# Probability-by-value product of the prompt attention: one head's high and low value columns as one stationary block, two matmuls per key tile in place of three

## Chip, cores and metric

The kernel runs on one core of one Trainium2 chip. The metric is device time in microseconds (us), from the first to the last instruction of one launch; the median of three runs before the change is 2038.55 us.

## What is computed

Two layers of a streaming encoder over 544 frames: 512 of a new prompt stream and 32 of a running stream. Each layer has a short convolution and a latent attention side by side, a gated merge, and a SwiGLU feed-forward part. The part that the change touches is the attention of the 512 prompt frames: 16 heads, 64 value columns each, masked in chunks of 64.

```python
kv = (c_all @ w_ukv).reshape(bsz, n_keys, N_HEADS, QK_NOPE + V_HEAD)
k_nope, v = kv[..., :QK_NOPE], kv[..., QK_NOPE:]
...
s = (jnp.einsum('bqhn,bkhn->bhqk', q_nope, k_nope)
     + jnp.einsum('bqhr,bkr->bhqk', q_rope, k_rope))
s = s.astype(jnp.float32) * ATTN_SCALE
mask = (k_pos // CHUNK)[None, :] <= (q_pos // CHUNK)[:, None]
s = jnp.where(mask[None, None], s, jnp.float32(NEG_INF))
p = jax.nn.softmax(s, axis=-1).astype(v.dtype)
return jnp.einsum('bhqk,bkhv->bqhv', p, v)
```

## The kernel before

Features lie on the 128 partitions and frames along the free axis, in two halves of 272 frames. Every float32 operand of a matmul is split into a high part of reduced precision (fp32r) and a low part that holds the rest. `split` (lines 128 to 130) does it in two steps: ScalarE copies the source into the high part, which rounds it, and VectorE subtracts that from the source into the low part. `mm3` (lines 183 to 186) then makes a product of three matmuls, low by high, high by low and high by high, all summed in one bank of PSUM.

One layer runs in stages: the input projection, the attention of the prompt frames with the convolution units woven in, the attention of the sample frames, the merge, and the feed-forward part. The order on TensorE, SyncE and GpSimd is the order in which the program is written. In the attention stages the order on VectorE and ScalarE is chosen by a scheduler when the program is built. An engine takes its instructions in order, so one that waits holds up all behind it.

The stage at hand is the loop over 16 heads (lines 781 to 805). For a head `k` the program issues on TensorE:

- `attn_s` for the query tiles 0 and 1 (scores of 128 queries by 256 keys), one `fill()`, then `attn_s` for the query tiles 2 and 3 (384 and 512 keys). `fill()` issues a unit of other work, 24 matmuls of 272 columns of a convolution or gate projection. The scores lie in the PSUM tiles `ps_s`, of which there are two, taken in turn. The softmax of a query tile goes: VectorE maximum (line 739), ScalarE exponential (742), VectorE reciprocal (744) and scaling (745) into a tile `pr`.
- `attn_t(0)`: three transposes of `pr` blocks into a bank `ps_t`; the first needs the scaled `pr` of query tile 1. `split` takes them to `pth` and `ptl`, the high and low parts of the transposed probabilities.
- in some heads, work for heads to come: `attn_v(k // 4)` (values of four heads), `prep_k`, `attn_group`; then `fill()`.
- `attn_t(1)` and `attn_t(2)`, four and three transposes, each followed by its `split`; in odd heads `prep_q` for the next pair; for the heads in `H` (line 448) another `fill()`. Heads 8 and 15 have nothing between `attn_t(2)` and the product.
- `attn_pv(k)` (lines 759 to 772), the product of probabilities and values. Two query pairs of 256 queries, of two and four key tiles; each of these six tiles is an `mm3`, 18 matmuls of 256 columns. The stationary block is the 128 columns of a pair of heads, of which only the 64 of head `k` are used: ScalarE copies those 64 partitions out of the bank `ps_v` into `at`.

```python
jj = (j % 2) * P
mm3(pv[:, qp * 256 : qp * 256 + 256], v[:, 0, kt, jj : jj + P], v[:, 1, kt, jj : jj + P],
    pth[:, b, o : o + 256], ptl[:, b, o : o + 256], kt == 0, kt == nkt - 1)
s = slice(64 * i, 64 * i + 64)
act.copy(at[0][s, j, :], pv[s, :TH])
act.copy(at[1][s, j, :PB], pv[s, TH:])
```

`attn_v(r)` (lines 686 to 699) makes the values of four heads for four key tiles: two banks `ps_d`, each with two key tiles of 256 columns, and one `split` of 512 columns for each bank. The banks `ps_d` are three and are taken in turn by all units in this stage, so a unit waits until the bank of the third unit before it has been read. Ahead of the head loop the order is `attn_v(0)`, two `fill()` units, `prep_k(0)`, `prep_q(0)`.

The pool `tp` (tag `t`) has six buffers for `pr` and other short-lived tiles.

Of the kernel before, what the change touches and what calls it, by code (L numbers as in the profile page):

```python
# [33 lines left out]
def kernel(  # L34
# [42 lines left out]
    def blk(shape, dt=F32, s="b"):  # L77
        return bp.tile(shape, dt, tag="b", name=nm(s))
# [49 lines left out]
    def split(hi, lo, src, eng_hi=None):  # L128
        act.copy(hi, src)  # L129
        dve.tensor_sub(lo, src, f32(hi))  # L130
# [52 lines left out]
    def mm3(ps, whi, wlo, xhi, xlo, first, last):  # L183
        pe.matmul(ps, lhsT=wlo, rhs=xhi, start=first, stop=False)  # L184
        pe.matmul(ps, lhsT=whi, rhs=xlo, start=False, stop=False)  # L185
        pe.matmul(ps, lhsT=whi, rhs=xhi, start=False, stop=last)  # L186
# [266 lines left out]
    for l in range(NL):  # L453
# [231 lines left out]

        def attn_v(r):
            wa = prep(w_a[l, r, :, 384:896], 512)
            v = blk([P, 2, 4, 256], F32R, "v")
            for t2 in range(2):
                ps = psd(512)  # L690
                for t in range(2):
                    tt = 2 * t2 + t
                    for k in range(2):
                        o = k * 256
                        mm3(ps[:, t * 256 : t * 256 + 256], c[:, 0, k, tt * P : tt * P + P], c[:, 1, k, tt * P : tt * P + P],
                            wa[:, 0, o : o + 256], wa[:, 1, o : o + 256], k == 0, k == 1)
                pr = ps.rearrange("p (t n) -> p t n", t=2)
                split(v[:, 0, 2 * t2 : 2 * t2 + 2, :], v[:, 1, 2 * t2 : 2 * t2 + 2, :], pr)
            vs[r] = v

        wbs = {}
# [57 lines left out]
        def attn_pv(k):  # L759
            j, i = k // 2, k % 2  # L760
            v = vs[j // 2]
            pv = bank("v")
            jj = (j % 2) * P
            for qp in range(2):
                nkt = 2 + 2 * qp
                for kt in range(nkt):
                    b, o = TB[(qp, kt)]
                    mm3(pv[:, qp * 256 : qp * 256 + 256], v[:, 0, kt, jj : jj + P], v[:, 1, kt, jj : jj + P],
                        pth[:, b, o : o + 256], ptl[:, b, o : o + 256], kt == 0, kt == nkt - 1)
            s = slice(64 * i, 64 * i + 64)  # L770
            act.copy(at[0][s, j, :], pv[s, :TH])
            act.copy(at[1][s, j, :PB], pv[s, TH:])

        attn_group(0)
        fill(F[2])
# [421 lines left out]
```

## Time and profile before

| what | us |
|---|---|
| runs (three) | 2038.04, 2038.55, 2038.92; median 2038.55 |
| span of the profiled execution | 2039.1 |
| TensorE busy in the span | 2012.5 (99%) |
| VectorE busy | 1126.1 (55%) |
| ScalarE busy | 826.2 (41%) |
| head loop of layer 0, about 115 to 353 us | 238 |
| head loop of layer 1, about 1127 to 1365 us | 238 |

The profiled execution's own time is its span, 2039.1 us, 0.55 us above the median of the runs. The busy time of an engine is the time in which at least one of its instructions was open. Matmuls overlap each other, so the pace of TensorE is read from the distance between the starts of neighbouring matmuls, not from their durations.

### The profile page before, as it was taken

Reading aid. Unit: us, or ns where it says so; the run is one execution under the profiler, and the core shown is the slowest. Engines: PE = TensorE matmul, PEld = TensorE weight load, DVE = VectorE, ACT = ScalarE, POOL = GpSimd, SP = SyncE. Lnnn points to the kernel's source line nnn. Section 1 sums busy time; section 2 is a strip of 40 time slices with the busy share of each in tenths; the row PEclk is TensorE's granted clock in tenths of the full one; section 3 lists DMA queues with packets and bytes.
Section 4 is the critical chain, followed back from the end, with each engine's and each line's share of the span. In section 5 each row is a group of like instructions: output and inputs, shape, how many; then the busy total and the mean of one; then the engine's idle time right before and its main releaser. Section 6 shows DMA issues by size and latency. Waiting matters only on the chain.

```text
span 2039.1 us, 37704 instructions
## 1 busy us (share of the span) xinstructions
PE 2012.5 (99%) x15780; PEld 1995.1 (98%) x15780; DVE 1126.1 (55%) x2330; ACT 826.2 (41%) x1692; POOL 89.6 (4%) x212
## 2 busy tenths in 40 slices
PE   8999999999999999999999999999999999999997
PEld 8999999999999999999999999999999999999997
DVE  7876775533457444432668776755334664444224
ACT  5455555622354222322444555546133533322231
POOL 0101000000000000000101100000000000000000
PEclk9999999999999999999999999999999999999998
DMA  5122222222342222233532222222223412222233
GB/s 190 63 76 67 68 71 78 80 97 94 106 148 95 73 93 84 84 92 90 183 104 77 64 64 74 82 73 92 94 83 115 157 66 83 92 88 88 78 113 125
DMA packets 58891, 190.93 MB, mean 94 GB/s; under 512 B 7970, under 2 KB 9666, under 8 KB 58594
## 3 DMA queue, kind: packets, MB, share of 16 engines
q1 hardware_dynamic: 49104, 163.58, 24.6%
q0 software_dynamic: 8320, 22.66, 3.4%
q8 instruction: 123, 2.02, 0.4%
q10 hardware_dynamic: 1296, 2.29, 0.3%
q14 instruction: 48, 0.38, 0.1%
HBM read 174.11 MB, written 10.20 MB: 90 GB/s over the span
## 4 chain that ended last, share of the span: by engine, by line
PE 93%; DVE 3%; DMA 1%; ACT 1%; issue 1%; SPq 0%; DVEq 0%; ACTq 0%
PE ps_d L184 16%; PE ps_d L186 16%; PE ps_d L185 16%; PE ps_s L184 7%; PE ps_s L186 7%; PE ps_s L185 7%; PE ps_t L184 6%; PE ps_t L186 6%; PE ps_t L185 6%; PE ps_t L755 2%; PE ps_v L185 1%; DMA raw<-in_w_in 1%; PE ps_v L186 1%; PE ps_v L184 1%; DVE w L130 1%
## 5 line engine op out<-in xcount | busy, mean ns | idle before, releaser
L130 DVE TENSOR_TENSOR w<-raw,w 128x1024 fp32r<-128x1024 f32 (+4 forms) x317 | 363.7, 1148 | 431.6 <-ACT w L129 429.5
L129 ACT CAST w<-raw 128x1024 fp32r<-128x1024 f32 (+4 forms) x317 | 312.1, 986 | 271.0 <-PE ps_d L186 107.8
L184 PE MATMUL ps_d<-hh,w 128*128 128x272 f32 x1080 | 315.2, 292 | 0.2
L185 PE MATMUL ps_d<-hl,w 128*128 128x272 f32 x1080 | 312.2, 289 | 0.8 <-DVE hl L314 0.8
L186 PE MATMUL ps_d<-hh,w 128*128 128x272 f32 x1080 | 312.4, 289 | 0.0
L184 PE MATMUL ps_d<-gh,w 128*128 128x272 f32 x704 | 205.9, 292 | 6.0 <-DVE w L130 5.8
L185 PEld LDWEIGHTS ps_d<-hl,w 128*128 128x128 f32 x1080 | 203.8, 189 | 2.0 <-DVE hl L314 1.3
L184 PEld LDWEIGHTS ps_d<-hh,w 128*128 128x128 f32 x1080 | 203.9, 189 | 1.5 <-PE ps_s L186 0.6
L186 PE MATMUL ps_d<-gh,w 128*128 128x272 f32 x704 | 204.4, 290 | 0.0
L186 PEld LDWEIGHTS ps_d<-hh,w 128*128 128x128 f32 x1080 | 203.4, 188 | 0.0
L185 PE MATMUL ps_d<-gl,w 128*128 128x272 f32 x704 | 203.4, 289 | 0.0
L184 PEld LDWEIGHTS ps_d<-gh,w 128*128 128x128 f32 x704 | 133.2, 189 | 6.5 <-DVE w L130 6.2
L184 PE MATMUL ps_s<-gh,w 128*128 128x272 f32 x464 | 136.9, 295 | 1.6 <-DVE w L130 1.6
L186 PE MATMUL ps_s<-gh,w 128*128 128x272 f32 x464 | 136.1, 293 | 0.0
L185 PE MATMUL ps_s<-gl,w 128*128 128x272 f32 x464 | 135.4, 292 | 0.0
L185 PEld LDWEIGHTS ps_d<-gl,w 128*128 128x128 f32 x704 | 133.5, 190 | 0.0
L186 PEld LDWEIGHTS ps_d<-gh,w 128*128 128x128 f32 x704 | 133.1, 189 | 0.0
L184 PE MATMUL ps_t<-gh,w 128*128 128x272 f32 x432 | 125.5, 291 | 0.0
L186 PE MATMUL ps_t<-gh,w 128*128 128x272 f32 x432 | 125.0, 289 | 0.0
L185 PE MATMUL ps_t<-gl,w 128*128 128x272 f32 x432 | 124.4, 288 | 0.0
L1045 ACT ACTIVATE sl<-sl 128x272 f32<-128x272 f32 x88 | 38.0, 432 | 182.9 <-DVE sl L1044 182.9
L1053 ACT CAST fh<-sl 128x272 fp32r<-128x272 f32 x88 | 36.9, 420 | 162.8 <-DVE sl L1051 162.8
(331 smaller groups left out, 5492.0 us busy)
## 6 DMA issues: line engine op xcount, KB each, us to landing
raw<-in_w_in SPq DMA_DIRECT2D x91, 512.0 KB, 3.4
raw<-in_w_gu SPq DMA_DIRECT2D x88, 512.0 KB, 3.3
raw<-in_w_mix SPq DMA_DIRECT2D x48, 512.0 KB, 3.2
raw<-in_w_dn SPq DMA_DIRECT2D x36, 512.0 KB, 3.6
raw<-in_w_dn SPq DMA_DIRECT2D x18, 384.0 KB, 3.1
raw<-in_w_b SPq DMA_DIRECT2D x16, 320.0 KB, 2.8
x_mid<-xb POOLq DMA_DIRECT2D x16, 272.0 KB, 2.3
xb<-x_mid POOLq DMA_DIRECT2D x16, 272.0 KB, 4.9
```

The source lines that it names most:

```text
L129: act.copy(hi, src)
L130: dve.tensor_sub(lo, src, f32(hi))
L184: pe.matmul(ps, lhsT=wlo, rhs=xhi, start=first, stop=False)
L185: pe.matmul(ps, lhsT=whi, rhs=xlo, start=False, stop=False)
L186: pe.matmul(ps, lhsT=whi, rhs=xhi, start=False, stop=last)
L755: pe.transpose(pt[:, o * P : o * P + P], probs[qt][:, kt * P : kt * P + P], ident)
L1045: act.activation(sl, sl, AF.Silu)
L1053: act.copy(fh[:, i % 8, :], sl)
```

## The change

The values of a head are laid out so that its 64 high and 64 low columns stand side by side: high then low for even heads, low then high for odd ones. This block of 128 columns is the stationary operand of both matmuls of a key tile, one over `ptl` and one over `pth`, so that four partial products (with low by low, which was left out before) come out of two matmuls. The high-column results lie on the same 64 partitions as before, the low-column results on the other 64. ScalarE copies the low 64 partitions, all 512 columns, to a new tile `rest` on the head's own partitions; VectorE adds `rest` to the high half in PSUM, in two pieces, into `at`. The first matmul of each key tile now reads `ptl`. In `attn_v` the split of a bank is done in two halves of 256 columns, one for each key tile.

```diff
         def attn_v(r):
             wa = prep(w_a[l, r, :, 384:896], 512)
-            v = blk([P, 2, 4, 256], F32R, "v")
+            v = blk([P, 4, 8, 64], F32R, "v")
+            vq = v.rearrange("p t (q a) d -> p t q a d", q=2)
             for t2 in range(2):
                 ps = psd(512)
...
-                pr = ps.rearrange("p (t n) -> p t n", t=2)
-                split(v[:, 0, 2 * t2 : 2 * t2 + 2, :], v[:, 1, 2 * t2 : 2 * t2 + 2, :], pr)
+                for t in range(2):
+                    pr = ps[:, t * 256 : t * 256 + 256].rearrange("p (q e d) -> p q e d", q=2, e=2)
+                    split(vq[:, 2 * t2 + t, :, 0::3, :], vq[:, 2 * t2 + t, :, 1:3, :], pr)
             vs[r] = v
...
             pv = bank("v")
-            jj = (j % 2) * P
+            a = 2 * (k % 4)
             for qp in range(2):
                 nkt = 2 + 2 * qp
                 for kt in range(nkt):
                     b, o = TB[(qp, kt)]
-                    mm3(pv[:, qp * 256 : qp * 256 + 256], v[:, 0, kt, jj : jj + P], v[:, 1, kt, jj : jj + P],
-                        pth[:, b, o : o + 256], ptl[:, b, o : o + 256], kt == 0, kt == nkt - 1)
-            s = slice(64 * i, 64 * i + 64)
-            act.copy(at[0][s, j, :], pv[s, :TH])
-            act.copy(at[1][s, j, :PB], pv[s, TH:])
+                    both = v[:, kt, a : a + 2, :]
+                    out = pv[:, qp * 256 : qp * 256 + 256]
+                    pe.matmul(out, lhsT=both, rhs=ptl[:, b, o : o + 256], start=kt == 0, stop=False)
+                    pe.matmul(out, lhsT=both, rhs=pth[:, b, o : o + 256], start=False, stop=kt == nkt - 1)
+            s, low = slice(64 * i, 64 * i + 64), slice(64 - 64 * i, P - 64 * i)
+            rest = tmp([P, NP], s="rest")
+            act.copy(rest[s, :], pv[low, :])
+            dve.tensor_add(at[0][s, j, :], pv[s, :TH], rest[s, :TH])
+            dve.tensor_add(at[1][s, j, :PB], pv[s, TH:], rest[s, TH:])
```

The scheduler gives VectorE and ScalarE another order with it. Two places matter below.

The first is VectorE at the beginning of head 2 of layer 0, with the last step of head 1. Line numbers after `attn_v` are shifted by 2 and, behind `attn_pv`, by 6: the maximum is L739 before and L741 after, the reciprocal L744 and L746, the scaling L745 and L747. Before:

```order
L739 TENSOR_REDUCE y_1690<-ps_s_237_1686 128x1
L744 RECIPROCAL y_1695<-y_1693 128x1
L739 TENSOR_REDUCE y_1702<-ps_s_242_1698 128x1
L745 TENSOR_SCALAR pr_1692<-pr_1692,y_1695 128x128
L744 RECIPROCAL y_1707<-y_1705 128x1
L745 TENSOR_SCALAR pr_1704<-pr_1704,y_1707 128x256
L604 TENSOR_TENSOR z_843<-cv_1537,ps_d_247_1710 128x240
L605 TENSOR_TENSOR z_843<-cv_1537,ps_d_247_1710 128x32
L739 TENSOR_REDUCE y_1741<-ps_s_248_1737 128x1
```

And after the change:

```order
L741 TENSOR_REDUCE y_1686<-ps_s_239_1682 128x1
L130 TENSOR_TENSOR slot_106_835<-ps_d_236_1649,slot_106_835 64x240
L777 TENSOR_TENSOR at_1114<-ps_v_237_1665,rest_1678 64x272
L778 TENSOR_TENSOR at_1115<-ps_v_237_1665,rest_1678 64x240
L746 RECIPROCAL y_1691<-y_1689 128x1
L741 TENSOR_REDUCE y_1698<-ps_s_244_1694 128x1
L747 TENSOR_SCALAR pr_1688<-pr_1688,y_1691 128x128
L604 TENSOR_TENSOR z_843<-cv_1537,ps_d_249_1706 128x240
L605 TENSOR_TENSOR z_843<-cv_1537,ps_d_249_1706 128x32
L746 RECIPROCAL y_1703<-y_1701 128x1
L741 TENSOR_REDUCE y_1737<-ps_s_250_1733 128x1
L747 TENSOR_SCALAR pr_1700<-pr_1700,y_1703 128x256
```

The two additions stand behind the maximum of query tile 0, and the scaling of query tile 1 (128x256) has moved from in front of the maximum of query tile 2 to behind it. That last move is found in heads 2, 6, 8, 12, 13 and 14 of both layers; in the other ten the scaling still stands in front.

The second is VectorE ahead of the head loop of layer 0, behind `attn_v(0)`, where the first bank is `ps_d_158` and `xr` is rotated in the lines 422 to 425. Before:

```order
L423 TENSOR_TENSOR sh_1144<-sh_1144,sinT 128x544
L424 TENSOR_TENSOR xr_1121<-xr_1121,cosT 128x544
L130 TENSOR_TENSOR v_1164<-ps_d_158_1165,v_1164 128x512
L130 TENSOR_TENSOR v_1164<-ps_d_159_1180,v_1164 128x512
L130 TENSOR_TENSOR w_1331<-raw_1330,w_1331 128x1024
L425 TENSOR_TENSOR xr_1121<-xr_1121,sh_1144 128x544
```

And after the change:

```order
L130 TENSOR_TENSOR v_1164<-ps_d_158_1165,v_1164 128x2x128
L423 TENSOR_TENSOR sh_1144<-sh_1144,sinT 128x544
L424 TENSOR_TENSOR xr_1121<-xr_1121,cosT 128x544
L130 TENSOR_TENSOR v_1164<-ps_d_159_1182,v_1164 128x2x128
L130 TENSOR_TENSOR w_1335<-raw_1334,w_1335 128x1024
L130 TENSOR_TENSOR v_1164<-ps_d_158_1165,v_1164 128x2x128
L425 TENSOR_TENSOR xr_1121<-xr_1121,sh_1144 128x544
```

The last read of the first bank now stands behind the subtraction for a weight tile (`w`, 1024 columns); before, it stood in front of it.

## Rows read from the trace of the kernel before

**Rows 1.** Page: span, TensorE's busy time, granted clock in 40 slices.

```profile
span 2039.1 us, 37704 instructions
...
PEclk9999999999999999999999999999999999999998
```

**Rows 2.** Groups of TensorE: count, busy us, mean ns of one, idle before.

```profile
L185 PE MATMUL ps_v<-ptl,v 128*128 128x256 f32 x192 | 54.7, 285 | 1.2 <-DVE ptl L130 1.2
```

**Rows 3.** Timeline of TensorE, head 2 of layer 0: start us, duration us.

```profile
146.97 0.28 PE L184 MATMUL ps_v<-pth,v 128*128 128x256 f32 x1
...
149.12 0.28 PE L184 MATMUL ps_s<-slot 128*128 128x256 f32 x1
```

**Rows 4.** Waits of TensorE, 60 to 400 us: total us, times, longest.

```profile
PE ps_d L185 <- DVE hl L314: 0.8, 2, 0.4
PE ps_v L185 <- DVE ptl L130: 0.6, 2, 0.3
PE ps_s L184 <- ACT prs L850: 0.3, 1, 0.3
```

**Rows 5.** Windows: the head loop of layer 0, and the beginning of layer 1.

```profile
115.00:353.00 238.00, 237.41 (x1836) 232.49 (x1835) 166.96 (x386) 131.97 (x335) 20.88 (x52) 1.00 0.24 72
...
1060.00:1120.00 60.00, 59.50 (x445) 58.48 (x445) 48.07 (x123) 27.63 (x60) 5.41 (x18) 0.94 0.20 65
```

**Rows 6.** Groups of ScalarE and VectorE by shape, 115 to 353 us.

```profile
L771 ACT COPY at<-ps_v 64x272 f32<-64x272 f32 x16 | 6.1, 380 | 18.3 <-PE ps_v L186 18.3
L772 ACT COPY at<-ps_v 64x240 f32<-64x240 f32 x16 | 5.7, 354 | 0.0
...
L129 ACT CAST v<-ps_d 128x512 fp32r<-128x512 f32 x6 | 3.5, 587 | 2.6 <-PE ps_d L186 2.6
...
L130 DVE TENSOR_TENSOR slot<-ps_d,slot 64x272 fp32r<-64x272 f32 x14 | 6.1, 436 | 1.5 <-ACT slot L129 1.3
...
L130 DVE TENSOR_TENSOR slot<-ps_d,slot 64x240 fp32r<-64x240 f32 x14 | 5.6, 402 | 0.3
```

**Rows 7.** Timelines of TensorE, then VectorE, head 14 of layer 0.

```profile
330.13 0.34 PE L184 MATMUL ps_s<-slot 128*128 128x384 f32 x1
...
331.36 0.38 PE L755 MATMUL ps_t<-ident,pr 128*128 128x128 f32 x2
...
328.79 0.41 DVE L739 TENSOR_REDUCE y<-ps_s 128x1 f32<-128x256 f32 x1
329.12 0.28 DVE L745 TENSOR_SCALAR pr<-pr,y 128x128 f32<-128x128 f32 x1
...
330.09 0.35 DVE L745 TENSOR_SCALAR pr<-pr,y 128x256 f32<-128x256 f32 x1
330.86 0.56 DVE L739 TENSOR_REDUCE y<-ps_s 128x1 f32<-128x384 f32 x1 [0.41 <-PE ps_s L186]
```

**Rows 8.** Timelines of TensorE, then VectorE, head 8 of layer 0.

```profile
242.27 0.36 PE L184 MATMUL ps_v<-pth,v 128*128 128x256 f32 x1
...
243.65 0.38 PE L185 MATMUL ps_v<-ptl,v 128*128 128x256 f32 x1 [0.30 <-DVE ptl L130]
243.87 0.28 PE L186 MATMUL ps_v<-pth,v 128*128 128x256 f32 x1
...
245.06 0.28 PE L184 MATMUL ps_s<-slot 128*128 128x256 f32 x1
...
242.90 1.16 DVE L130 TENSOR_TENSOR ptl<-ps_t,pth 128x512 fp32r<-128x512 f32 x2 [0.67 <-ACT pth L129]
```

**Rows 9.** Timelines of TensorE, then VectorE, ahead of the head loop of layer 0.

```profile
96.32 0.29 PE L184 MATMUL ps_d<-hh,w 128*128 128x272 f32 x1
...
93.52 0.70 DVE L423 TENSOR_TENSOR sh<-sh,sinT 128x544 f32<-128x544 f32 x1
...
94.80 1.27 DVE L130 TENSOR_TENSOR v<-ps_d,v 128x512 fp32r<-128x512 f32 x2
95.99 1.20 DVE L130 TENSOR_TENSOR w<-raw,w 128x1024 fp32r<-128x1024 f32 x1
```

## The prediction

> **What bounds the kernel now.** I read the page first. TensorE is busy almost all of the 2039.1 us, and its granted clock stands at the upper of its two levels, 2.4 GHz, in nearly every slice [rows 1]. So what counts is TensorE's pace and its waits, and other engines only where TensorE waits for them. Next the groups by line: the product of probabilities and values is 192 matmuls of 256 columns for each of the three partial products [rows 2]. Their duration of 285 ns is not their price, since they overlap. The timeline of one head gives that: from the first of its 18 matmuls to the first of the next scores 149.12 - 146.97 = 2.15 us pass, 0.119 us for each [rows 3]. Then the waits of TensorE: from 60 to 400 us it waited less than 2 us in all, and one of the three rows lies inside the product, 0.3 us in each of two heads, for the last low parts of the probabilities [rows 4]. Last the window of the head loop: VectorE is the next engine, busy 167.0 of 238 us, ScalarE 132.0 [rows 5]. VectorE has room on average, so the question is whether it is late at the one moment when TensorE needs it.
>
> **The change part by part.**
>
> Removed: one matmul of three for 6 key tiles, 16 heads and 2 layers, that is 192 [rows 2]. At 0.119 us each [rows 3] this is 192 x 0.119 = **22.9 us** (2.15 / 3 = 0.72 us per head). Ends: the pace is a measured one for just this shape, so I allow 22 to 23.5.
> The Trainium skill has another price: "TensorE: Matmul & The Clock Gate", section "Back-to-back issue gap", gives a stream of weight load and matmul pairs 81 ns at 128 columns and 131 ns at 512; an estimate on the straight line between them is 98 ns at 256 columns, with which the matmuls would be worth 18.8 us and the sum below would be 18.8 - 5.8 - 1.4 - 1.5 = 10.1 us gained, about 2028.4. The row of this case, 0.119 us, does not agree and decides.
>
> Evictions of the product: ScalarE gives up two copies of 0.380 and 0.354 us [rows 6] and does one of 64x512, for which the nearest row is 0.587 us (128x512 out of PSUM). VectorE gets two additions with one operand in PSUM; the nearest rows, subtractions of the same shapes, take 0.436 and 0.402 us [rows 6], a little less than 0.8 us a head, under 13 us a layer. VectorE has 238 - 167 = 71 us free [rows 5], so I cost them at nothing as work. The copy moves data to other partitions, which no row shows; its bounds are nothing extra and twice the 0.587. ScalarE's copy and the additions read `ps_v`, whose next use is a head later, about 15 us: nothing there either way. If that cover went, for example because VectorE was late by 1 us in every head, the softmax behind it would be the one to tell.
>
> That is where the order of VectorE counts. In head 2 as in heads 6, 8, 12, 13 and 14 of both layers, 12 places, the scaling of query tile 1 now stands behind the maximum of query tile 2 (front, first place). The first transpose needs that scaling. Head 14 shows the times [rows 7]: the scores of query tile 2 start at 330.13, their maximum can start only at 330.86, and TensorE wants the transpose at 331.36. The scaling was started at 330.09 and was long done. Now it starts when the maximum lets go: rows of such pairs show the next instruction start 0.08 us before the end of the one before (328.79 + 0.41 against 329.12), so 330.86 + 0.56 - 0.08 = 331.34, and it ends at 331.34 + 0.35 = 331.69. TensorE is late by 0.33 us, plus the resumption: in head 8 a matmul that had waited was followed after 0.22 us (243.65 to 243.87) [rows 8], not 0.119, so 0.10 more, and 0.05 for the signal, which I estimate from the same row (243.65 is a few hundredths behind the end of the first of the two subtractions). Together 0.48 us, 12 x 0.48 = **5.8 us lost**. Ends: 12 x 0.33 = 4.0 without resumption; 12 x 0.85 = 10.2 if VectorE has another 0.37 us of backlog there (about one addition). I take the middle one because the maximum itself waits for TensorE, which swallows backlog before it.
>
> Heads 8 and 15 of both layers have no cover between the last transposes and the product. In head 8 the product starts at 242.27 and stops until 243.65, 1.38 us later, for the low part [rows 8]. The new order reads that low part with the first matmul of the third key tile, and 1.38 us is still when it is there. Before, 11 matmuls were left (243.65 to 245.06), now 8. So this head saves 3 x 0.119 = 0.36 us and not 0.72: 4 x 0.36 = **1.4 us lost**. Ends: nothing, if VectorE is earlier there, and 0.72 each, 2.9 us, if it is later by 0.36.
>
> Values: each bank is split in two halves. The copy of 512 columns takes 0.587 us and one of 272 columns 0.380 [rows 6], so a split bank costs ScalarE some 0.15 us more, VectorE likewise; in heads 4, 8 and 12 other units of TensorE cover that. Ahead of the head loop they don't: the second half of the first bank is now read behind the subtraction of a 1024-column weight tile (front, second place). From 93.52 [rows 9]: one half about 0.34, the two rotations 94.80 - 93.52 = 1.28, another half 0.34, the weight tile 1.2, the second half 0.42; the bank is free at about 97.1, and the second `fill()` unit, third in turn on this bank, was started at 96.32. That is 0.75 us with the signal, in each layer: **1.5 us lost**. Ends: nothing, if the weight tile's subtraction waits less than I think and the half goes first in time, and 2.4 us, if ScalarE's second copy is late by another 0.45.
>
> The rest of each layer keeps its instructions and only starts earlier. SyncE's and GpSimd's order is the same as before apart from buffer names, and the weight transfers wait for the buffers that VectorE and ScalarE free, so they move with the rest. The new tile `rest` takes one of six buffers of `tp`; the buffers it presses on hold `pr` tiles that the transposes have released before the product starts, so I cost it at nothing, up to 2 us.
>
> **The sum.** 22.9 - 5.8 - 1.4 - 1.5 = 14.2 us gained. On the profiled execution, 2039.1, that is 2024.9; the median of the runs is 0.55 lower, so **2024.4 us**, 0.7% less. TensorE's clock falls to its lower level, 1.2 GHz, for short stretches at the layers' beginnings (the window at 1060 us shows 0.94 [rows 5]); if layer 1 begins 7 us earlier these may fall otherwise, and I leave 2 us to both sides for it. A difference of 0.2%, 4 us, is about what a measurement of this kernel can tell from no change.
>
> **Rivals.**
>
> *The scaling is never late*: the maximum or the transposes shift so that the 5.8 us don't appear. For it speaks that VectorE has 30% of the loop free; against it that the maximum of query tile 2 can't start before its scores, and that this leaves 0.50 us (330.86 to 331.36) for 0.83 us of work [rows 7]. Time: 2024.4 - 5.8 = 2018.6.
>
> *VectorE is late in more heads*: its additions, which wait for the end of the product and ScalarE's copy, stand in front of the reciprocal and maximum of query tile 1 in 30 heads. If half the heads lose another 0.4 us to it at the transposes or in front of the product, 16 x 0.4 = 6.4 us, the time is 2030.8. For it: the low parts decide already in four heads. Against: the scaling of query tile 1 ended at 330.44, 0.9 us ahead of its transpose [rows 7].
>
> *Slower than before*: the copy across partitions and the additions become the bound of the softmax. It decides from the point where every head loses over 0.72 us at its first transpose; the scaling of query tile 1 has 0.9 us to spare in head 14 [rows 7], so it would have to come over 1.6 us later. The additions bring 0.8 of that, so the copy would have to take over 0.8 us more than the 0.587 of its nearest row. With 2.0 us for it the scaling comes 0.8 + 1.4 = 2.2 us later, a head loses 2.2 - 0.9 = 1.3 us and saves 0.72: 32 x 0.58 = 18.6 us slower, 2057.
>
> *It does not do what it says*: the matmuls go but TensorE's time is taken by something that hides behind them, and nothing over 0.2% is left. Against it: the loop's 0.6 us of idle time in 238 [rows 5]. Time: 2036.
>
> **How the numbers follow.** My forecast, 2021 to 2028, has a chance of 0.62; the scaling never late 0.12; more heads late 0.18; no gain to speak of 0.05; slower 0.03. The range from 2018 to 2031 takes in the first three cases: at the lower end 5.8 us of waits fall away, at the upper the transposes' wait is at its 10.2 and the other bounds at theirs, 22.9 - 10.2 - 2.9 - 2.4 = 7.4, 2031.2. Faster by over 0.2%: 0.92; within 0.2%: 0.05; slower: 0.03.
>
> **What the profile would show.** Right: 192 matmuls fewer, still 0.119 us apart; waits of TensorE at line 757 (the transposes) for VectorE's scaling, some 0.3 us each in 12 places; four waits of a product's low-part matmul, longer than 0.3 us; one wait of a `fill()` unit in front of the head loop for the subtraction of `v`, 0.7 us, in each layer; VectorE busier by 12 us a loop, the head loop some 7 us shorter. Wrong: no waits at line 757, or such waits in nearly all heads; new waits at `ps_s` for the exponential; or a loop whose matmuls are further apart.

## The result and the profile after

The changed kernel takes 2023.38 us (median of 4 runs, 2021.93 to 2026.63), against 2038.74 of the kernel before in the same comparison: a ratio of 0.9923, interval 0.9909 to 0.9937, 15.4 us less. The forecast was 2024.4, in a range from 2018 to 2031. The profiled execution is the longest of the four; its span, from the first to the last instruction in the profile, is 2024.6 us and its time 2026.63. The part ahead took a span for the time of a run; where a run has both on record, the time is 1.7 to 2.9 us more. The forecast does not hang on this, since 2024.9 - 0.55 is the median of the runs before, 2038.55, less the 14.2 of the sum.

The waits of TensorE over its whole span are the first view (us in total, times, longest), to be held against [rows 4]:

```profile
PE ps_v L772 <- DVE ptl L130: 2.5, 4, 0.7
...
PE ps_t L757 <- DVE pr L747: 1.6, 8, 0.2
PE ps_d L184 <- DVE v L130: 1.3, 2, 0.7
...
PE ps_s L184 <- ACT pr L744: 0.4, 2, 0.2
```

The first three are the three waits of the forecast: the product for the low parts in heads 8 and 15, the transposes for VectorE's scaling, the unit ahead of the loop for the values. Each comes in both layers; at the transposes there are eight waits of 0.2 us and not twelve of 0.3. The fourth is new: it is in head 14 of each layer, and the forecast had named such waits, of `ps_s` for the exponential, as a sign of being wrong. The groups of 115 to 345.7 us, by shape, answer to [rows 2, 6]:

```profile
L772 PE MATMUL ps_v<-ptl,v 128*128 128x256 f32 x96 | 24.0, 286 | 1.3 <-DVE ptl L130 1.3
L773 PE MATMUL ps_v<-pth,v 128*128 128x256 f32 x96 | 23.7, 282 | 0.0
...
L776 ACT COPY rest<-ps_v 64x512 f32<-64x512 f32 x16 | 9.3, 582 | 11.1 <-PE ps_v L773 10.7
L777 DVE TENSOR_TENSOR at<-ps_v,rest 64x272 f32<-64x272 f32 x16 | 6.9, 434 | 1.5 <-ACT rest L776 1.4
L778 DVE TENSOR_TENSOR at<-ps_v,rest 64x240 f32<-64x240 f32 x15 | 6.0, 397 | 0.0
```

The copy to other partitions, which no row showed before, takes 582 ns, about as long as its nearest row (587). The additions take 434 and 397, as the subtractions of the same shapes (436 and 402). VectorE and TensorE in head 14 of layer 0, the counterpart of [rows 7]:

```profile
322.68 0.42 DVE L741 TENSOR_REDUCE y<-ps_s 128x1 f32<-128x256 f32 x1
323.02 0.28 DVE L747 TENSOR_SCALAR pr<-pr,y 128x128 f32<-128x128 f32 x1
323.80 0.16 DVE L746 RECIPROCAL y<-y 128x1 f32<-128x1 f32 x1 [0.50 <-ACT pr L744]
323.88 0.54 DVE L741 TENSOR_REDUCE y<-ps_s 128x1 f32<-128x384 f32 x1
324.33 0.34 DVE L747 TENSOR_SCALAR pr<-pr,y 128x256 f32<-128x256 f32 x1
```

```profile
322.95 0.34 PE L184 MATMUL ps_s<-slot 128*128 128x384 f32 x1
...
323.82 0.50 PE L184 MATMUL ps_s<-slot 128*128 128x512 f32 x1 [0.19 <-ACT pr L744]
...
324.73 0.55 PE L757 MATMUL ps_t<-ident,pr 128*128 128x128 f32 x3
325.03 0.37 PE L184 MATMUL ps_d<-hh,w 128*128 128x272 f32 x1
```

From the scores of query tile 2 to the transposes 324.73 - 322.95 = 1.78 us pass; before it was 1.23 [rows 7]. The scaling ends at 324.67, and the transposes start 0.06 us later, as the forecast has it. But the rows show one more wait, that of the scores of query tile 3 (128x512) for the exponential of query tile 1: these matmuls take the bank that the exponential reads. Head 14 is the exception: the same distance is 1.59 or 1.60 us in heads 2, 6, 8, 12 and 13 of both layers, and 1.22 in the other ten. Head 8, TensorE, answers to [rows 8]:

```profile
238.33 0.36 PE L772 MATMUL ps_v<-ptl,v 128*128 128x256 f32 x1
...
239.65 0.39 PE L772 MATMUL ps_v<-ptl,v 128*128 128x256 f32 x1 [0.60 <-DVE ptl L130]
239.87 0.28 PE L773 MATMUL ps_v<-pth,v 128*128 128x256 f32 x1
...
240.70 0.28 PE L184 MATMUL ps_s<-slot 128*128 128x256 f32 x1
```

The product starts 3.94 us earlier than before and the next scores 4.36, so this head saves 0.42 us and not 0.72. Ahead of the loop, VectorE and TensorE, beside [rows 9]:

```profile
95.24 1.20 DVE L130 TENSOR_TENSOR w<-raw,w 128x1024 fp32r<-128x1024 f32 x1
...
96.38 0.41 DVE L130 TENSOR_TENSOR v<-ps_d,v 128x256 fp32r<-128x256 f32 x1
```

```profile
96.93 0.36 PE L184 MATMUL ps_d<-hh,w 128*128 128x272 f32 x1 [0.66 <-DVE v L130]
```

The second half of the first bank is read behind the weight tile, and the unit starts at 96.93; before it was 96.32, in a run that had come to this place 0.2 us later.

**How kernels are compared below.** The whole times of one kernel's runs lie up to 7.2 us apart (`e_third_back`, 2038.69 to 2045.9). Windows of two profiled executions of the changed kernel show why (the column in front of the last two is TensorE's mean granted clock), first of the one above, then of its repetition `c_after`:

```profile
1060.00:1080.00 20.00, 20.00 (x139) 20.00 (x139) 17.31 (x55) 5.95 (x12) 0.46 (x4) 0.83 0.01 1
```

```profile
1060.00:1080.00 20.00, 20.00 (x167) 20.00 (x166) 19.10 (x61) 6.87 (x15) 0.77 (x5) 1.00 0.08 27
```

With the same program, TensorE ran part of this window at its lower level, 1.2 GHz, and issued 139 matmuls in it, or all of it at 2.4 and issued 167. Between 104 and 338 us and between 1114 and 1340 us, most of the two head loops, the clock is 1.00 in every profile of this study, and in the one repetition the loops came back within 0.05 us. So I measure two lengths from TensorE's rows: a **loop**, from the start of the first scores to the end of the last product matmul, and a **lead**, from the first matmul of the first values to the first scores. The changed kernel's loop of layer 0 runs from 103.64 to 344.94.

| kernel | ratio to before, interval | loops, layers 0 and 1 | leads |
|---|---|---|---|
| before | 1 | 249.57, 250.28 | 12.59, 12.59 |
| changed | 0.9923, 0.9909 to 0.9937 | 241.30, 241.39 | 13.41, 13.42 |
| `c_after` | 0.9922, 0.9908 to 0.9935 | 241.30, 241.35 | 13.42, 13.42 |
| `e_scale_first` | 0.9907, 0.9892 to 0.9922 | 239.40, 239.46 | 13.43, 13.40 |
| `e_one_split` | 0.9924, 0.9912 to 0.9937 | 241.44, 242.38 | 12.59, 12.60 |
| `e_high_first` | 0.9919, 0.9906 to 0.9933 | 240.60, 240.72 | 13.43, 13.41 |
| `e_third_back` | 1.0011, 1.0002 to 1.0019 | 249.58, 249.68 | 13.41, 13.40 |
| `e_no_add` | 0.9891, 0.9877 to 0.9904 | 238.66, 238.63 | 13.41, 13.40 |
| `e_max_first` | 0.9969, 0.9959 to 0.9978 | 245.78, 245.79 | 13.41, 13.41 |
| `e_late_add` | 0.9913, 0.9900 to 0.9927 | 240.59, 240.60 | 13.40, 13.42 |
| `e_one_defer` | 0.9915, 0.9901 to 0.9930 | 241.41, 242.06 | 12.59, 12.59 |
| `e_best` | 0.9890, 0.9877 to 0.9904 | 238.33, 239.03 | 12.58, 12.60 |
| `e_best_cover` | 0.9932, 0.9918 to 0.9945 | 243.48, 243.97 | 12.58, 12.60 |
| `e_best_table` | 0.9882, 0.9866 to 0.9899 | 238.36, 238.48 | 12.59, 13.22 |

Loops and leads together went from 525.03 to 509.52 with the change, 15.5 us less, which is the whole gain of 15.4. Verdicts on small edits rest on these lengths, since the intervals of the ratios overlap.

### The profile page after: what moved, and what is told of

Read it like the earlier page. It is cut to its first block, busy times and chain, and to the rows that moved or that the text cites. A ratio compares the mean times of both kernels' runs of the same rounds, so it can differ in the third digit from the quotient of the medians.

```text
span 2024.6 us, 37375 instructions
## 1 busy us (share of the span) xinstructions
PE 1992.8 (98%) x15588; PEld 1970.8 (97%) x15588; DVE 1147.1 (57%) x2410; ACT 827.2 (41%) x1676; POOL 85.7 (4%) x212
## 4 chain that ended last, share of the span: by engine, by line
PE 93%; DVE 4%; DMA 1%; ACT 1%; issue 1%; SPq 0%; DVEq 0%; ACTq 0%
PE ps_d L184 16%; PE ps_d L186 16%; PE ps_d L185 16%; PE ps_s L184 7%; PE ps_s L186 7%; PE ps_s L185 7%; PE ps_t L184 6%; PE ps_t L186 6%; PE ps_t L185 6%; PE ps_t L757 2%; DMA raw<-in_w_in 1%; PE ps_v L772 1%; PE ps_v L773 1%; DVE w L130 1%; ACT w L129 1%
```

## The experiments

**The changed kernel again** (`c_after`, no edit).

> The changed kernel once more, nothing edited, as the measure for the other three. Its four runs so far lie between 2021.93 and 2026.63 us, median 2023.38. Theory one (the places and sizes of the waits are fixed by the order of the instructions): every wait at the transposes, at the product of heads 8 and 15 and at the unit ahead of the loop comes back within 0.05 us, and the runs differ only in the stretches at the lower clock, so the median is 2022 to 2025. Rival (the spread of 4.7 us comes from the new waits, which are a race between VectorE and TensorE): some of the twelve waits at the transposes are missing or double in this run's trace.

The median was 2022.68. All waits came back: eight at the transposes, four at the product, two at the unit ahead of the loop, in total 1.6, 2.5 and 1.3 us, as above. Theory one holds. Loops and leads of the two executions sum to 509.52 and 509.49 us, while their spans are 4.3 us apart. TensorE's rows show 2.9 of these 4.3 us between 1065.4 and 1072.1 us of the first, where matmuls of 272 columns start 0.23 us apart and in the second run 0.125: the spread is the clock's.

**The order of scaling and maximum** (`e_scale_first`).

```diff
...
-            dve.tensor_reduce(mx, ps[:, :nk], axis=AX.X, op=ALU.max, negate=True)
+            with (tc.issue_after(scaled[1]) if qt == 2 else nullcontext()):
+                dve.tensor_reduce(mx, ps[:, :nk], axis=AX.X, op=ALU.max, negate=True)
...
-            dve.tensor_scalar_mul(pr[:, :nk], pr[:, :nk], rs)
+            scaled[qt] = dve.tensor_scalar_mul(pr[:, :nk], pr[:, :nk], rs).ins
```

> The scaling of query tile 1 is queued in front of the maximum of query tile 2 on VectorE in every head; that differs from the changed kernel in heads 2, 6, 8, 12, 13 and 14 of both layers. Theory one (the order of these two costs 0.46 us in each of twelve places, mean of the trace): no wait left at the transposes, 12 x 0.46 = 5.5 us less, 2017.9 by the median of 2023.38. Rival A (the maximum of query tile 2, now later, sends its exponential and all behind it late): half the gain or less, 2020.6 or more, with new waits at the scores of query tile 3 or at the last transposes. Rival B (the transposes wait for VectorE's additions in front, not for this order): the waits stay, 2023.

The waits at the transposes are gone from the list, yet the loops are shorter by 1.90 and 1.89 us, 3.8 in all and not 5.5. From a head's first scores to those of the next, heads 2, 8, 12 and 13 got back 0.30 to 0.46 us each, heads 6 and 14 only 0.15 to 0.21. VectorE and then TensorE in head 14 of this kernel show what is left there:

```profile
321.32 0.44 DVE L778 TENSOR_TENSOR at<-ps_v,rest 64x272 f32<-64x272 f32 x1
321.67 0.41 DVE L779 TENSOR_TENSOR at<-ps_v,rest 64x240 f32<-64x240 f32 x1
...
322.30 0.42 DVE L742 TENSOR_REDUCE y<-ps_s 128x1 f32<-128x256 f32 x1
...
323.62 0.35 DVE L748 TENSOR_SCALAR pr<-pr,y 128x256 f32<-128x256 f32 x1
323.89 0.55 DVE L742 TENSOR_REDUCE y<-ps_s 128x1 f32<-128x384 f32 x1
```

```profile
322.58 0.34 PE L184 MATMUL ps_s<-slot 128*128 128x384 f32 x1
...
323.44 0.50 PE L184 MATMUL ps_s<-slot 128*128 128x512 f32 x1 [0.17 <-ACT pr L745]
...
324.24 0.49 PE L758 MATMUL ps_t<-ident,pr 128*128 128x128 f32 x3
```

The scaling ends at 323.97, in time for 324.24. The delay is now the scores of query tile 3: the two additions stand in front of the maximum of query tile 1 (322.30), so its exponential lets go of the bank too late. Rival A had a wait at these scores, but from the later maximum of query tile 2; it is that of query tile 1, and the additions stand in front of it; in head 14 the changed kernel had this wait already.

**Without additions** (`e_no_add`).

```diff
-            rest = tmp([P, NP], s="rest")
-            act.copy(rest[s, :], pv[low, :])
-            dve.tensor_add(at[0][s, j, :], pv[s, :TH], rest[s, :TH])
-            dve.tensor_add(at[1][s, j, :PB], pv[s, TH:], rest[s, TH:])
+            act.copy(at[0][s, j, :], pv[s, :TH])
+            act.copy(at[1][s, j, :PB], pv[s, TH:])
```

> On top of the changed kernel (2022.68, loops 241.30 and 241.35): the product is evicted as before the change, by two copies of ScalarE; the additions of VectorE are left out and with them the low part of the values. With fewer instructions the scaling of query tile 1 stands in front of the maximum of query tile 2 in all heads again. Theory one (with the scaling first, 0.75 us of each loop is still lost, in heads 6 and 14, since the additions stand in front of the maximum of query tile 1 and the scores of query tile 3 wait for its exponential): loops 239.4 - 0.75 = 238.65, time 2022.68 - 2 x 2.65 = 2017.4. Rival A (what is left in heads 6 and 14 comes from the splits of the queries that stand there too): loops 239.4, 2018.9. Rival B (the additions also delay the low parts that heads 8 and 15 wait for): loops under 238.2, 2016.5 or less.

Loops 238.66 and 238.63, time 2017.41: theory one. Against the scaling first, head 6 comes back by 0.26 us and head 14 by 0.43. In head 14 the maximum of query tile 1 now starts 0.82 us ahead of the scores of query tile 2 (it was 0.28), and the wait is gone:

```profile
321.43 0.42 DVE L741 TENSOR_REDUCE y<-ps_s 128x1 f32<-128x256 f32 x1
```

```profile
322.25 0.34 PE L184 MATMUL ps_s<-slot 128*128 128x384 f32 x1
...
322.77 0.39 PE L184 MATMUL ps_s<-slot 128*128 128x512 f32 x1
```

So the order gives back 3.8 us, and the additions after it another (239.40 - 238.66) + (239.46 - 238.63) = 1.6 us: 1.4 in heads 6 and 14, and 0.12 us each in head 2. The other 26 heads gain nothing beyond 0.05 us. These are not two shares of one loss, since the delays overlap: in the changed kernel head 6 has its transposes 1.59 us behind the scores of query tile 2, as heads 2, 8, 12 and 13 have, though its scores of query tile 3 are 0.16 us late and theirs are not.

**The order made worse** (`e_max_first`).

```diff
-            dve.tensor_reduce(mx, ps[:, :nk], axis=AX.X, op=ALU.max, negate=True)
+            peak[qt] = dve.tensor_reduce(mx, ps[:, :nk], axis=AX.X, op=ALU.max, negate=True).ins
...
-            dve.tensor_scalar_mul(pr[:, :nk], pr[:, :nk], rs)
-            probs[qt] = pr
+            probs[qt] = (pr, rs, nk)
+            for t in {1: (), 2: (1, 2)}.get(qt, (qt,)):
+                pr, rs, nk = probs[t]
+                with (tc.issue_after(peak[2]) if t == 1 else nullcontext()):
+                    dve.tensor_scalar_mul(pr[:, :nk], pr[:, :nk], rs)
+                probs[t] = pr
```

> On top of the changed kernel (2022.68, loops 241.30 and 241.35): on VectorE the scaling of query tile 1 is queued behind the maximum of query tile 2 in all 32 heads and not in 12. Theory one (this order costs a head 0.37 us, the mean of what heads 2, 8, 12 and 13 got back with the scaling first, since the maximum can't start before its scores): 20 x 0.37 = 7.4 us more, loops 245.0, time 2030.1; up to 0.46 for each, 2031.9. Rival A (it costs only where VectorE is already behind with other work): less than 2 us more, loops under 242.3, under 2025. Rival B (the late exponential of query tile 1 and the maximum add up in all heads as in head 14): 0.55 each, 2033.7.

Loops 4.48 and 4.44 us longer, 20 places at 0.45 (0.41 to 0.48): theory one, at its upper value. The time, 2033.62, is Rival B's, but Rival B's 0.55 in each head is in none of the 20; the ratios of this run and `c_after` are 0.47% apart, 9.6 us, close to the 8.9 of the loops. Every head added loses 0.38 us at its first transposes, and most another 0.07 behind it. In the list of waits the eight at the transposes have become 28:

```profile
PE ps_t L761 <- DVE pr L751: 5.9, 28, 0.2
```

In these 20 heads the order costs the same, whatever else VectorE has to do there.

**The additions in the next head** (`e_late_add`, on top of the scaling first).

```diff
...
+                top = dve.tensor_reduce(mx, ps[:, :nk], axis=AX.X, op=ALU.max, negate=True).ins
+            while qt == 2 and adds:
+                with tc.issue_after(top):
+                    adds.pop()()
...
-            dve.tensor_add(at[0][s, j, :], pv[s, :TH], rest[s, :TH])
-            dve.tensor_add(at[1][s, j, :PB], pv[s, TH:], rest[s, TH:])
+            def add():
+                dve.tensor_add(at[0][s, j, :], pv[s, :TH], rest[s, :TH])
+                dve.tensor_add(at[1][s, j, :PB], pv[s, TH:], rest[s, TH:])
+            adds.append(add)
+            if k == 15:
+                adds.pop()()
```

> On top of the kernel with the scaling first (2019.76, loops 239.40 and 239.46): the two additions of a head are issued in the next head, queued behind the maximum of its query tile 2; nothing is left out. Theory one (the additions cost only because they stand in front of the maximum of query tile 1 in heads 6 and 14): loops 238.65, as without additions, time 2019.76 - 1.5 = 2018.3. Rival A (in the new place they delay the low parts of the first transposes or the scaling of query tile 2, and the next transposes or the product wait): loops 239.4 or more, with new waits at the transposes or at the product's low-part matmuls, 2020 or more. Rival B (the splits of the queries decide in heads 6 and 14): loops 239.4, 2019.8, no new waits.

Rival A. Heads 6 and 14 come back (0.26 and 0.43 us) with nothing left out, which says that it was the place of the additions that cost there, but heads 1 and 8 lose 1.05 and 0.89: there the additions push the scalings of query tiles 2 and 3 back, other work of VectorE gets in front of the last one, and the second transposes wait:

```profile
PE ps_t L761 <- DVE pr L751: 3.0, 4, 0.8
```

Moving the work in all heads because two of them need it costs more than it brings. `e_best` moves the additions of heads 5 and 13 alone.

**One split for each bank** (`e_one_split`). The new layout allows it: for two key tiles the pairs of heads lie 256 columns apart.

```diff
-            vq = v.rearrange("p t (q a) d -> p t q a d", q=2)
...
-                for t in range(2):
-                    pr = ps[:, t * 256 : t * 256 + 256].rearrange("p (q e d) -> p q e d", q=2, e=2)
-                    split(vq[:, 2 * t2 + t, :, 0::3, :], vq[:, 2 * t2 + t, :, 1:3, :], pr)
+                pr = ps.rearrange("p (q e d) -> p q e d", q=4, e=2)
+                vq = v[:, 2 * t2 : 2 * t2 + 2].rearrange("p t (q a) d -> p (t q) a d", q=2)
+                split(vq[:, :, 0::3, :], vq[:, :, 1:3, :], pr)
```

> The values of two key tiles are split in one step of 512 columns for each bank, as before the change, into the new layout; all else as changed. Theory one (the second half of the first bank is read late, behind the weight tile, and holds the second fill unit up by 0.81 us in each layer): that wait goes, 1.6 us less, 2021.8. Rival A (the bank is late by the weight tile's subtraction whatever the split): the wait stays, 2023.4. Rival B (ScalarE and VectorE also save some 0.3 us in heads 4, 8 and 12 of each layer, and head 8 gains from it): another 0.3 us in head 8 of each layer, 2021.2.

Both leads fall to 12.59 and 12.60, the value before the change, so the wait was the split's. But the loops grow by 0.14 and 1.03 us, which no theory had. The waits from 1100 to 1350 us and ScalarE at head 0 of layer 1:

```profile
PE ps_s L184 <- ACT pr L743: 0.8, 3, 0.4
```

```profile
1109.01 0.35 ACT L129 CAST slot<-ps_d 64x240 fp32r<-64x240 f32 x1
1109.38 1.28 ACT L743 ACT_TABLE_LOAD   x1
1110.67 0.37 ACT L743 ACTIVATE pr<-ps_s,y 128x128 f32<-128x128 f32 x1
```

In layer 1 the first exponential needs its table loaded, 1.28 us. With this order of ScalarE, which is that of the kernel before, all evictions of the first queries stand in front of the load, and head 0 loses 0.65 us more than in layer 0, most of it at the scores of query tile 3. The kernel before had the same wait of 0.39 us, and the changed kernel does not: its scheduler put the last eviction behind the exponential. Of the rest, 0.12 us are in head 0 of each layer, as in the kernel before, and another 0.24 us are in head 6 of layer 1, whose scores of query tile 3 start 0.28 us later for a reason that stays open. In loops and leads together 0.5 us are won.

**Those evictions behind the exponential** (`e_one_defer`).

```diff
...
-                for i in range(2):
+                def out(i, hf=hf, n=n, ps=ps):
...
+                out(0)
+                if j == 0:
+                    held.append(out)
+                else:
+                    out(1)
...
+            while k == 0 and qt == 0 and held:
+                with tc.issue_after(ex):
+                    held.pop(0)(1)
```

> On top of the kernel with one split for each bank (the stretch from the first values to the first scores 12.59 and 12.60 us, loops 241.44 and 242.38): the evictions of the first query projection into the slot of head 1 are issued behind the first exponential of head 0, so that ScalarE loads the table of the exponential before them. Theory one (in layer 1 these copies stand in front of the table load of 1.28 us, the exponential of query tile 1 is late and the scores of query tile 3 wait 0.39 us for it, as in the kernel before; the values' wait of 0.81 us had only hidden that): loops 241.3 and 241.35, the first stretches stay at 12.6, so by the changed kernel 2022.68 - 2 x 0.82 = 2021.0. Rival (the exponential is late because everything ahead of it runs earlier by 0.8 us, and the wait stays at whatever place the copies have): loop of layer 1 over 242, 2022.

In between: the scores no longer wait, as in theory one, but the loop of layer 1 is 242.06, the number of the rival, 0.65 us longer than that of layer 0. VectorE's part of the moved evictions now stands in front of the scaling of query tile 1, and the first transposes come 0.34 us late.

**High parts first** (`e_high_first`).

```diff
-                for kt in range(nkt):
-                    b, o = TB[(qp, kt)]
...
+                for n, src in enumerate((pth, ptl)):
+                    for kt in range(nkt):
+                        b, o = TB[(qp, kt)]
+                        pe.matmul(pv[:, qp * 256 : qp * 256 + 256], lhsT=v[:, kt, a : a + 2, :], rhs=src[:, b, o : o + 256],
+                                  start=n == 0 and kt == 0, stop=n == 1 and kt == nkt - 1)
```

> In the product, for each query pair, the matmuls with the high parts of the probabilities come first and those with the low parts last; the count is the same. It matters where the low parts are late, heads 8 and 15 of both layers. Theory one (two waits in a row: the low part of the bank of transposes 2 is written 1.78 us behind the product's start, and two matmuls and the resumption must follow it, so the next scores start 2.13 us behind it and not 2.37): 0.24 us in four places, 1.0 us less, 2022.4. Rival A (only the first late low part counts, and four matmuls of 0.119 us move in front of it): 4 x 0.48 = 1.9 us less, 2021.5. Rival B (the high part of the last bank, ready 0.92 us behind the start, becomes a wait of its own and the low part's is no shorter): no gain, 2023.4.

Theory one. Head 8, TensorE:

```profile
237.81 0.48 PE L771 MATMUL ps_v<-pth,v 128*128 128x256 f32 x2
238.13 0.40 PE L771 MATMUL ps_v<-ptl,v 128*128 128x256 f32 x2
238.41 0.89 PE L771 MATMUL ps_v<-pth,v 128*128 128x256 f32 x4
239.13 0.97 PE L771 MATMUL ps_v<-ptl,v 128*128 128x256 f32 x4
239.94 0.28 PE L184 MATMUL ps_s<-slot 128*128 128x256 f32 x1
```

The next scores start 239.94 - 237.81 = 2.13 us behind the product's start, as worked out, and heads 8 and 15 come back by about 0.25 us each. The loops gain 0.70 and 0.63 us; another 0.19 of it is in head 14, where VectorE's order happened to change.

**The third matmul back** (`e_third_back`, on top of the scaling first).

```diff
                     pe.matmul(out, lhsT=both, rhs=ptl[:, b, o : o + 256], start=kt == 0, stop=False)
+                    pe.matmul(out, lhsT=both, rhs=ptl[:, b, o : o + 256], start=False, stop=False)
```

> On top of the kernel with the scaling first (2019.76; its two head loops, from the first scores to the end of the last product, take 239.40 and 239.46 us in its trace): the matmul with the low parts of the probabilities is issued twice, so that a key tile has three matmuls again. The output holds the low part of the probabilities twice. Theory one (a matmul costs its distance, 0.119 us, and nothing hides it): 16 x 6 x 0.119 = 11.4 us for each loop, of which heads 8 and 15 hide two matmuls, 0.24 each, in their wait, and up to 0.75 us is won back where VectorE's additions were late; loops 249.6 to 250.4, the time 2040 to 2042, so no better than before the change. Rival A (a matmul of this shape costs 0.098 us): 9.4 us less 0.4 for each loop, 248.4, 2038. Rival B (the gain did not come from the matmuls, but from the copies that ScalarE no longer does): loops under 243, 2025.

Theory one: 2041.02 us, loops 249.58 and 249.68. The start of the product and of the next scores, head 2 of layer 0:

```profile
147.55 0.28 PE L773 MATMUL ps_v<-ptl,v 128*128 128x256 f32 x1
147.67 0.28 PE L774 MATMUL ps_v<-ptl,v 128*128 128x256 f32 x1
...
149.71 0.28 PE L184 MATMUL ps_s<-slot 128*128 128x256 f32 x1
```

(149.71 - 147.55) / 18 = 0.120 us for each. The loops are those of the kernel before in layer 0 (249.57), so all of the gain is matmul count, and with three matmuls the rest of the change, even with the scaling first, leaves the kernel 0.1% slower than it was. The estimate of 0.098 us that the forecast worked out from the Trainium skill ("TensorE: Matmul & The Clock Gate", section "Back-to-back issue gap") is not borne out by this row.

**All that paid** (`e_best`): the edits of `e_scale_first`, `e_one_split`, `e_one_defer` and `e_high_first`, and the additions of two heads late.

```diff
+            adds.append(add)
+            if k not in (5, 13):
+                adds.pop()()
```

> All that paid, together: scaling of query tile 1 in front of the maximum of query tile 2; the additions of heads 5 and 13 alone behind that maximum of the next head; high parts first in the product; one split for each bank of values; the first query evictions behind the first exponential. Nothing is left out. Theory one (the costs are separate waits of TensorE and add up): loops as without additions, 238.65, less 2 x 0.25 for heads 8 and 15 = 238.15; first stretches 12.6; by the changed kernel 2022.68 - 2 x 3.2 - 2 x 0.82 = 2014.6. Rival (TensorE, freed of one wait, meets the next one: the splits and weight tiles that VectorE still has to do): loops over 239, 2017 or more.

In between. The loop of layer 0 is 238.33 (forecast 238.15) and the leads are 12.58 and 12.60: there the waits of the scaling, the additions, the split and the low parts add up as separate costs. The loop of layer 1, 239.03, and the time, 2018.68 us (a ratio of 0.9890), are the rival's, but its place is head 0, as in `e_one_defer`, and not the splits and weight tiles that the rival named. In lengths it is 7.0 us less than `c_after`, against 8.0 forecast; the two ratios are 0.32% apart, 6.5 us.

**Cover for heads 8 and 15** (`e_best_cover`).

```diff
-    H = (0, 2, 3, 4, 6, 9, 10, 12, 14)
+    H = (0, 2, 4, 6, 8, 10, 12, 14, 15)
```

> The combination, and two of the nine units of other work that stand in front of the product are moved, from heads 3 and 9, where the low parts are ready 3.4 us ahead of the product, to heads 8 and 15, where they come 1.7 us behind its start. The count of units is the same. Theory one (heads 8 and 15 wait for want of cover, 2.13 us from the product's start to the next scores in place of 1.43): 0.70 us in four places, loops 238.15 - 1.4 = 236.75, 2014.6 - 2.8 = 2011.8. Rival A (the moved units' evictions and weights come at other times and make VectorE late at the transposes of heads 3 to 9): new waits at the transposes, loops 238 or more, 2014 or more. Rival B (heads 3 and 9 lose what 8 and 15 win): loops 238.15.

Rival A. The product's wait in heads 8 and 15 is shorter by 0.69 and 0.75 us, as forecast, but both lose part or all of it again ahead of the product, and head 6 loses 1.9 us, head 14 1.3 and head 13 1.1; the loops are 5 us longer. New waits for VectorE's scaling stand at the transposes; that they come from the work that the moved units bring for VectorE was not tested by itself:

```profile
PE ps_t L770 <- DVE pr L760: 6.5, 8, 1.6
```

**The table load alone** (`e_best_table`), in place of `e_one_defer`'s edit.

```diff
+        if l:
+            tc.keep_in_program_order(act.activation(tiny([P, 1]), ones[:, 0:1], AF.Exp))
         prep_k(0)
         prep_q(0)
```

> The combination (loops 238.33 and 239.03, the two stretches from the first values to the first scores 12.58 and 12.60) without the moved query evictions; in their place, in layer 1, an exponential of one column is issued at the beginning of the attention, so that its table is loaded there. Theory one (the 0.70 us by which the loop of layer 1 is longer than that of layer 0 is the table load of 1.28 us in front of the first exponential of head 0, which ScalarE does in no other head): loop of layer 1 238.3, all else as it was, 0.7 us less than the combination, 2018.0. Rival A (the load in its new place holds up the latents or the values: the stretch from the first values to the first scores grows): over 13.0 in layer 1, no gain. Rival B (in head 0 of layer 1 something else is late): loop of layer 1 stays at 239.0.

Both: the loop of layer 1 falls to 238.48, next to layer 0's 238.36, though the evictions of the first queries stand in front of the first exponential as in `e_one_split`; so the table load was what made it longer. But the lead of layer 1 grows from 12.60 to 13.22, as Rival A has it, and nothing is won. The ratio, 0.9882, can't be told from `e_best`'s 0.9890.

## Why the prediction was right

Measured in the traces of the two kernels, by the prediction's own terms:

| term | predicted | measured |
|---|---|---|
| 192 matmuls | 22.9 | 23.0: 32 x 0.72; 0.120 each in `e_third_back` |
| first transposes, 12 places | -5.8 | -5.6: 0.41 to 0.62 each |
| heads 8 and 15 | -1.4 | -1.3: they save 0.42 and 0.37, not 0.72 |
| leads | -1.5 | -1.65: 0.82 in layer 0, 0.83 in layer 1 |
| head 0 | none | +0.9: 0.12 in layer 0, 0.79 in layer 1 |
| sum | 14.2 | 15.4, and 15.5 by the lengths |

**The price of a matmul** was right because it was read from the distance of starts in just this shape [rows 3]. Its duration of 285 ns [rows 2] would have given 55 us.

**The transposes** were right in place and size, 0.46 us on average against 0.48, and the mechanism is the one that was told: `e_scale_first` takes the waits away and `e_max_first` makes them in 20 more heads. The step that does not hold everywhere is that the maximum of query tile 2 "waits for TensorE, which swallows backlog before it". In heads 6 and 14 the additions, behind an eviction of queries, make the exponential of query tile 1 late, and the scores of query tile 3 wait for their bank. In head 6 the order hides this; in head 14, whose rows the forecast was worked out from, it adds 0.19 us (1.78 against 1.59). That is the forecast's rival "VectorE is late in more heads", in few places, and only with the order put right does the rest come out: `e_scale_first` gains 3.8 us and not 5.5, `e_no_add` another 1.6. That the twelve places sum to nearly the forecast's 5.8 is in part luck: they hold a delay in head 14 that was not foreseen, and elsewhere 0.41 to 0.47 us, a little less than the 0.48 reckoned.

**Heads 8 and 15** went as worked out: 1.32 us after the start of the product the low part is there (1.38 before), and eight matmuls are left.

**The lead** is 0.07 us longer than forecast in each layer, and that is a slip in the sum: the forecast's own terms give 97.1 - 96.32 = 0.78 us, and 0.83 with its 0.05 for the signal, where it wrote 0.75. `e_one_split` takes the whole of it away, though 0.12 us come back in head 0 of each layer and more in layer 1.

**The failing step** is "the rest of each layer keeps its instructions and only starts earlier". ScalarE's order in head 0 of layer 1 changed too, the table load went in front of the last eviction, and a wait that the kernel before had there fell away. First that wait, from the list of the kernel before, then ScalarE in the changed kernel (`c_after`):

```profile
PE ps_s L184 <- ACT pr L742: 0.4, 1, 0.4
```

```profile
1105.96 1.28 ACT L744 ACT_TABLE_LOAD   x1
1107.26 0.37 ACT L744 ACTIVATE pr<-ps_s,y 128x128 f32<-128x128 f32 x1
...
1107.79 0.36 ACT L129 CAST slot<-ps_d 64x240 fp32r<-64x240 f32 x1
```

Head 0 of layer 1 gains 0.67 us more by it than head 0 of layer 0; `e_one_split`, with the order of before, loses it again. It was to be seen: the wait stands in that list, and ScalarE's order could have been read as VectorE's was. The 0.7 us lie inside the 2 us that the range left for the clock; with the 0.12 us in head 0 of each layer, for which the sum had no term either, they are most of the difference between 14.2 and 15.5.

**The rival "slower than before"** fell with the copy across partitions: 0.582 us, where it needed over 1.4 and was priced with 2.0. **"The scaling is never late"** fell with the eight waits, and **"It does not do what it says"** with the loops, shorter by 8.3 and 8.9 us.

## What to carry to other kernels

On an engine that is 99% busy, as TensorE is here, a removed instruction is worth the distance between starts, and all of it where the engine does not wait (0.72 us a head, and 0.42 and 0.37 in heads 8 and 15); what the change puts on other engines is then looked for at the few moments when the busy engine waits for them, not in their busy share: VectorE had 71 us free in a loop [rows 5] and still made TensorE lose 2.8 us at the transposes in it, most of that by the order of two instructions. An order that a scheduler makes is part of the change: read it on every engine, and pin the two or three pairs that a waiting engine depends on. Moving work out of the way should be done only where it is in the way; done everywhere, it found new waits (`e_late_add`, `e_best_cover`).

## What the runs showed that I had not expected

- The same program, without any edit, spends a different number of stretches at the lower granted clock from run to run (0.83 and 1.00 in the same window), which set the spans of two executions 4.3 us apart, over a quarter of this change's gain. The runs of `e_third_back` lie 7.2 us apart. In both runs TensorE does 24 matmuls of one column there (line 237, from 1063.37 and from 1062.11 us); at 1065.40 their starts go from 0.11 to 0.21 us apart in the one run, whose clock falls, and in the other, which stays at 2.4 GHz, they keep to 0.11. What decides it stays open.
- A table load of ScalarE, 1.28 us in head 0 of layer 1 alone, decides whether TensorE waits for the second exponential (`e_one_split`, `e_best_table`). The Trainium skill ("ScalarE: Activation LUTs", section "What ACT_TABLE_LOAD costs") gives 1283 ns for the load and about 1380 ns more for a drain. The trace agrees with the first; of the second it shows nothing here: in `e_one_split` the load starts 0.02 us behind the eviction in front of it, and the exponential starts as it ends (1109.38 + 1.28 = 1110.66, 1110.67).
- A copy of 64 partitions to the other 64 costs ScalarE nothing extra that these rows show: 582 ns for 512 columns, against 587 for 512 columns that stay on their partitions [rows 6].
